# One up tile per chunk gets its exact rest from an accumulating transfer instead of a VectorE subtraction

## The chip, the cores and the metric

The kernel runs on one core of a Trainium2 chip. The metric is the device time of one execution, in microseconds. The core has five engines that run their own instruction queues in order and wait for each other through semaphores: TensorE (PE, matmuls; PEld is its weight load), VectorE (DVE), ScalarE (ACT), GpSimd (POOL) and SyncE (SP). SyncE, ScalarE and GpSimd can issue transfers, which 16 DMA engines carry out.

## The reference

Two layers of a residual trunk over 256 tokens of width 2048, in float32. Each layer has a mixer (two groups of attention heads between an input and an output projection) and a feed-forward part. The change touches the feed-forward part only:

```
h = rms_norm(x, pre_ffn_norm[l])                       # 256 x 2048
f = (silu(h @ w_gate[l]) * (h @ w_up[l])) @ w_down[l]  # 2048 -> 5632 -> 2048
x = x + rms_norm(f, post_ffn_norm[l])
```

## The kernel before

Every product is made of rounded parts. A float32 matrix W is split into hi, W rounded to TensorE's reduced format (float32r), and lo = W - hi, the exact rest, which fits that format too. With the activations split in the same way (sh, sl), a product is three matmuls: sh hi, sh lo, sl hi (`product`, lines 922 to 927).

All weights lie in DRAM in the order in which they are used (`weight_order`, `weights_laid_out`), as tiles of 128 partitions by 2 by 512 float32 values, 512 KB each. `fetch` (line 184) issues the loads on SyncE's queue into one of four `raw` buffers (line 202); `feed` (line 240) splits a tile, with ScalarE rounding it to `hi` (line 250) and VectorE subtracting (line 252, `lo`). `hi` and `lo` have six buffers each. `weights(i, ahead)` feeds four tiles ahead of the one that TensorE is to use (LOOKAHEAD = 4).

Gate and up: the 5632 hidden columns are cut into 11 chunks (c = 0 to 10) of 512. In each chunk the 2048 rows are taken as eight row pairs kp of 256 rows, and each pair has a gate tile and an up tile, so a chunk uses 16 tiles: gate and up of kp 0, then of kp 1, and so on. Four of the row pairs (kp 2, 4, 5 and 6; 4 and 6 in chunk 0) are done by `seven`, a 2-by-2 block product with seven instead of eight block products. Its up tile `T` is the sum of the up tile and half of the gate tile; that sum is made by a transfer: the up tile is loaded by SyncE (line 210), and GpSimd then issues a transfer that adds the first half of the gate tile to it on its way into the buffer (line 211, `accum_op`, 256 KB). `mixed_weights` (lines 216 to 238) makes the further sums on VectorE (lines 232, 233) and splits them (lines 225, 226, into `Th`, `Tl`, `hi`, `lo`). The other four row pairs are done by `eight` (line 1035), 24 matmuls with the plain `hi` and `lo` of the gate and up tiles. Row pair 1, which the change concerns, is one of these, from chunk 1 on in every chunk.

At the end of a chunk, `shared_part` (lines 959 to 966) combines what the seven products share (ScalarE line 962, VectorE lines 963 to 966) out of the banks of PSUM that the next chunk then needs, and lines 1079 to 1082 apply SiLU, the row scale and the product of gate and up. The results are transposed on TensorE some ticks later (`flip`, line 1084).

The order of the instructions on each engine is made when the kernel is built: a scheduler lists the instructions by priorities, and each engine then runs its list in order. A wait at the head of a list holds everything behind it. GpSimd's list in this stage holds nothing but the accumulating transfers; SyncE's holds the loads.

Of the kernel before, what the change touches and what calls it, by code (L numbers as in the profile page):

```python
# [10 lines left out]
F32R = mybir.dt.float32r  # L11
BF16 = mybir.dt.bfloat16
AF = mybir.ActivationFunctionType
ALU = mybir.AluOpType
# [3 lines left out]
P = 128  # L18
D = 2048
S = 256  # L20
L = 2
# [3 lines left out]
FF = 5632  # L25
CW = 512
# [29 lines left out]
def weight_order():  # L56

    order = []

    def queue_pair(name, l, kp, c):  # L60
        order.append((name, l, kp, c))
        return len(order) - 1

    plan = []
    sevens, plain = set(), set()
    for l in range(L):
        lay = {"in": {}, "o": {}, "gate": {}, "up": {}, "down": {}}
        for n, (ca, cb) in enumerate(PAIRS):
            for kp in IN_ORDER if n else range(KT // 2):
                lay["in"][ca, kp] = queue_pair("w_in", l, kp, ca)  # L70
                lay["in"][cb, kp] = queue_pair("w_in", l, kp, cb)
                if kp in IN_NOW[n]:
                    plain.add(lay["in"][cb, kp])
        order_o = [(c, kp) for kp in KP_O for c in (0, 1)]
        order_o += [(c, kp) for c in (2, 3) for kp in range(KT // 2)]
        lay["order_o"] = order_o
        for c, kp in order_o:
            lay["o"][c, kp] = queue_pair("w_o", l, kp, c)
        for c in range(FF // CW):
            for kp in FIRST_ORDER if c == 0 else range(KT // 2):  # L80
                lay["gate"][c, kp] = queue_pair("w_gate", l, kp, c)
                lay["up"][c, kp] = queue_pair("w_up", l, kp, c)
                if kp in (FIRST_SEVEN if c == 0 else SEVEN):
                    sevens.add(lay["up"][c, kp])
        for half in range(2):
            for kp in range(FF // P // 2):
                for c in (2 * half, 2 * half + 1):
                    lay["down"][c, kp] = queue_pair("w_down", l, kp, c)
                if kp in DOWN_SEVEN:
                    sevens.add(lay["down"][2 * half + 1, kp])  # L90
        plan.append(lay)
    return order, plan, sevens, plain
# [48 lines left out]
def kernel(  # L141
# [15 lines left out]
    nc = tc.nc  # L157
    const = ctx.enter_context(tc.tile_pool(name="const", bufs=1))
    small = ctx.enter_context(tc.tile_pool(name="small", bufs=4))
    wpool = ctx.enter_context(tc.tile_pool(name="wpool", bufs=1))  # L160
# [14 lines left out]


    order, plan, sevens, plain = weight_order()
    stream = [weights_in_turn[i].rearrange("p (k n) -> p k n", k=2) for i in range(len(order))]

    ready = {}  # L180
    raws, loads = [], []
    fed = [0]

    def fetch(upto):
        while len(raws) < min(upto, len(stream)):
            i = len(raws)
            for j in range(i, min(i + EARLY + 1, mix_raw[3])):
                if j in sevens and j not in sums:
                    summed(j)
            if i in sevens:  # L190
                raws.append(sums[i])
                continue
            if i + 1 in sevens:
                g = mix_raw[0].tile([P, 2, CW], F32, tag="G", bufs=mix_raw[1], name=f"G{i}")
                loads.append(nc.sync.dma_start(g, stream[i]))
                raws.append(g)
                continue
            if i in plain or i + 1 in plain:
                raw = mix_pool[0].tile([P, 2, CW], F32, tag="GU", bufs=4, name=f"GU{i}")
            else:  # L200
                raw = wpool.tile([P, 2, CW], F32, tag="raw", bufs=4, name=f"raw{i}")
            loads.append(nc.sync.dma_start(raw, stream[i]))
            raws.append(raw)
# [3 lines left out]
    def summed(i):  # L207

        sums[i] = mix_raw[0].tile([P, 2, CW], F32, tag="T", bufs=mix_raw[2], name=f"T{i}")
        loads.append(nc.sync.dma_start(sums[i], stream[i]))  # L210
        nc.gpsimd.dma_start(sums[i][:, 0, :], stream[i - 1][:, 0, :], accum_op=ALU.add)  # L211
# [4 lines left out]
    def mixed_weights(i):  # L216

        g, u = raws[i - 1], raws[i]
        hi = wpool.tile([P, 2, CW], F32R, tag="hi", bufs=6, name=f"hi{i}")
        lo = wpool.tile([P, 2, CW], F32R, tag="lo", bufs=6, name=f"lo{i}")  # L220
        th = mix_pool[0].tile([P, 3, CW], F32R, tag="Th", bufs=1 if i in plain else 2, name=f"Th{i}")
        tl = mix_pool[0].tile([P, 3, CW], F32R, tag="Tl", bufs=1 if i in plain else 2, name=f"Tl{i}")

        def split(h, l, w):
            nc.scalar.activation(h, w, AF.Copy)  # L225
            nc.vector.tensor_tensor(out=l, in0=w, in1=h.bitcast(F32), op=ALU.subtract)  # L226

        if i in plain:
            nc.vector.tensor_tensor(out=u[:, 0, :], in0=g[:, 0, :], in1=u[:, 0, :], op=ALU.add)
        split(hi, lo, u)  # L230
        t2 = u[:, 1, :]
        nc.vector.tensor_tensor(out=t2, in0=t2, in1=u[:, 0, :], op=ALU.subtract)  # L232
        nc.vector.tensor_tensor(out=g, in0=g, in1=t2.unsqueeze(1).to_broadcast([P, 2, CW]), op=ALU.add)  # L233
        split(th[:, 2, :], tl[:, 2, :], t2)
        split(th[:, 0:2, :], tl[:, 0:2, :], g)
        t1, b22 = ((hi[:, k, :], lo[:, k, :]) for k in range(2))
        t3, t4, t2 = ((th[:, k, :], tl[:, k, :]) for k in range(3))
        return {"b22": b22, "t1": t1, "t2": t2, "t3": t3, "t4": t4}

    def feed(upto):  # L240
        fetch(upto)
        while fed[0] < min(upto, len(stream)):
            i = fed[0]
            raw = raws[i]
            if i in sevens or i in plain:
                ready[i] = mixed_weights(i)
                fed[0] += 1
                continue
            hi = wpool.tile([P, 2, CW], F32R, tag="hi", bufs=6, name=f"hi{i}")
            nc.scalar.activation(hi, raw, AF.Copy)  # L250
            lo = wpool.tile([P, 2, CW], F32R, tag="lo", bufs=6, name=f"lo{i}")
            rest = nc.vector.tensor_tensor(out=lo, in0=raw, in1=hi.bitcast(F32), op=ALU.subtract)  # L252
            ready[i] = (hi, lo)
            fed[0] += 1
            rests.append(rest)
# [11 lines left out]
    def weights(i, ahead):  # L267
        feed(i + 1 + ahead)
        return ready[i]
# [702 lines left out]
    for l in range(L):  # L972
# [29 lines left out]
        with tc.manual_schedule(engines={mybir.EngineType.Activation, mybir.EngineType.DVE}):  # L1002
            feed(idx + 6)
            for kp in range(4, 8):
                unit(accs, mix, idx + kp - 4, kp, (0,), False, kp == 7, 0)
            evac_chunk(pool, accs[0], mg, ssm, gpost, 3, 0, f"o{l}")
            rescale(mg, ssm, 0, f"o{l}")
            for kp in range(4, 8):
                feed(idx + 3 + kp)
                fetch(min(idx + 8 + kp, idx + 12))  # L1010
                unit(accs, mix, idx + kp - 4, kp, (1,), False, kp == 7, 0)
                transposed(0, 32 + l * KT, xT, cols=(kp - 4,))
# [90 lines left out]
        for half in range(2):  # L1103
# [69 lines left out]
            for t in range(NT):  # L1173
# [4 lines left out]
                for c in cc:  # L1178
                    for kp in range(nkp - tail, nkp):
# [3 lines left out]
                        hi, lo = weights(plan[l]["down"][c, kp], LOOKAHEAD)  # L1183
# [67 lines left out]
```

## Time and profile before

| | |
|---|---|
| time, median of 3 runs | 2214.32 us (2211.67 to 2216.69) |
| profiled execution | 2215.14 us, span 2213.4 us, granted clock 0.998 |
| busy in the span | TensorE 99%, VectorE 84%, ScalarE 61%, GpSimd 6% |
| transfers | 466.73 MB, mean 211 GB/s |
| subtraction lo (line 252), from raw tiles | 534 times, mean 1223 ns |
| rounding hi (line 250), from raw tiles | 534 times, mean 1053 ns |
| issue of an accumulating transfer (line 211) | 108 times, mean 873 ns; lands after 3.7 / 6.7 / 9.4 us (least, median, most) |
| load of a 512 KB raw tile | 534 times, lands after 4.7 us (median) |

How to read the profile: busy time is the time in which an engine has an instruction at work; instructions are pipelined, so two that follow each other closely overlap a little. A releaser, written after an arrow, is what ended an idle time. The DMA share is how much of the time the 16 DMA engines had a packet at work, on average.

### The profile page before, as it was taken

To read this page: it belongs to the slowest core of one execution; us is meant where nothing else is said; L and a number is where in the kernel's file an instruction comes from. 1 tells how busy PE (TensorE), PEld (TensorE's weight loads), DVE (VectorE), ACT (ScalarE), POOL (GpSimd) and SP (SyncE) were. 2 spreads that over 40 slices of the span, in tenths; PEclk is the share of its full clock that TensorE was granted. 3 is DMA by queue.
4 is the path that set the end of the run, shared out by engine and by line. 5 is a ranking of instruction groups with operands and counts; after the bars stand their busy time and mean duration, and the time that the engine had idled before them with its cause. 6 is when DMAs were issued, how large, how long until landed. Compare 5 with 4: busy or idle time off the path is not lost.

```text
span 2213.4 us, 28454 instructions
## 1 busy us (share of the span) xinstructions
PE 2185.5 (99%) x10009; PEld 1790.9 (81%) x10009; DVE 1864.0 (84%) x2548; ACT 1354.6 (61%) x2030; POOL 142.2 (6%) x184
## 2 busy tenths in 40 slices
PE   9999999999999999999999999999999999999998
PEld 7788888778888888888888888887788888888886
DVE  7888655899999998989788886559999999999897
ACT  7566664656656656656565656646666556566564
POOL 1200000000000000000011000000000000000000
PEclk9999999999999999999999999999999999999999
DMA  8654555776776775767465545558677677667672
GB/s 304 208 180 153 190 176 186 250 237 215 218 256 211 211 258 180 241 215 240 157 239 190 177 160 177 174 187 268 208 225 235 224 221 238 226 204 243 200 254 98
DMA packets 138079, 466.73 MB, mean 211 GB/s; under 512 B 15824, under 2 KB 16336, under 8 KB 137424
## 3 DMA queue, kind: packets, MB, share of 16 engines
q1 hardware_dynamic: 120512, 430.30, 56.3%
q0 software_dynamic: 15552, 28.32, 7.5%
q10 hardware_dynamic: 1872, 6.31, 0.7%
q8 instruction: 78, 1.28, 0.2%
q14 instruction: 65, 0.53, 0.1%
HBM read 456.47 MB, written 8.39 MB: 210 GB/s over the span
## 4 chain that ended last, share of the span: by engine, by line
PE 78%; DVE 11%; DMA 4%; issue 3%; ACT 3%; SPq 0%; DVEq 0%; ACTq 0%
PE c L925 7%; PE c L926 7%; PE c L927 7%; PE in L925 5%; PE in L927 5%; PE in L926 5%; PE dn L1136 5%; PE dn L1135 5%; PE dn L1138 5%; DVE lo L252 3%; DMA raw<-in_weights_in_turn_dram 3%; PE o L464 3%; PE o L466 3%; PE o L465 3%; DVE Tl L226 2%
## 5 line engine op out<-in xcount | busy, mean ns | idle before, releaser
L252 DVE TENSOR_TENSOR lo<-raw,hi 128x1024 fp32r<-128x1024 f32 x534 | 643.3, 1223 | 161.4 <-ACT hi L250 161.2
L250 ACT ACTIVATE hi<-raw 128x1024 fp32r<-128x1024 f32 x534 | 552.4, 1053 | 235.1 <-DMA raw<-in_weights_in_turn_dram 63.5
L925 PE MATMUL c<-hi,xF 128*128 128x512 f32 x820 | 321.8, 395 | 6.2 <-DVE w L966 4.0
L926 PE MATMUL c<-lo,xF 128*128 128x512 f32 x820 | 320.0, 391 | 0.0
L927 PE MATMUL c<-hi,xF 128*128 128x512 f32 x820 | 318.3, 390 | 0.0
L211 POOL DMA_DIRECT2D T<-in_weights_in_turn_dram x108 | 94.3, 873 | 1669.3 <-PE c L926 520.9
L925 PEld LDWEIGHTS c<-hi,xF 128*128 128x128 f32 x820 | 153.7, 188 | 40.8 <-DVE w L966 6.3
L1135 PE MATMUL dn<-hi,jh 128*128 128x512 f32 x464 | 180.7, 389 | 0.0
L1136 PE MATMUL dn<-lo,jh 128*128 128x512 f32 x464 | 180.5, 389 | 0.0
L926 PEld LDWEIGHTS c<-lo,xF 128*128 128x128 f32 x820 | 154.1, 188 | 32.0 <-DVE lo L252 1.6
L927 PEld LDWEIGHTS c<-hi,xF 128*128 128x128 f32 x820 | 153.9, 188 | 32.1
L252 DVE TENSOR_TENSOR lo<-G,hi 128x1024 fp32r<-128x1024 f32 x108 | 131.7, 1220 | 26.7 <-ACT hi L250 26.6
L225 ACT ACTIVATE Th<-T 128x512 fp32r<-128x512 f32 x108 | 67.8, 627 | 138.6 <-DVE T L232 126.7
L1138 PE MATMUL dn<-hi,jl 128*128 128x512 f32 x464 | 142.9, 389 | 0.0
L226 DVE TENSOR_TENSOR lo<-T,hi 128x1024 fp32r<-128x1024 f32 x108 | 131.7, 1220 | 10.9 <-ACT hi L225 10.3
L226 DVE TENSOR_TENSOR Tl<-G,Th 128x1024 fp32r<-128x1024 f32 x108 | 131.8, 1220 | 9.6 <-ACT Th L225 9.6
L225 ACT ACTIVATE hi<-T 128x1024 fp32r<-128x1024 f32 x108 | 113.4, 1050 | 40.4 <-PE c L927 19.9
L225 ACT ACTIVATE Th<-G 128x1024 fp32r<-128x1024 f32 x108 | 113.9, 1054 | 36.6 <-DVE G L233 35.2
L233 DVE TENSOR_TENSOR G<-G,T 128x1024 f32<-128x1024 f32 x108 | 132.0, 1222 | 2.1
L925 PE MATMUL in<-hi,xT 128*128 128x512 f32 x328 | 131.5, 402 | 0.5 <-ACT hi L738 0.5
L925 PE MATMUL in<-hi,xI 128*128 128x512 f32 x328 | 131.3, 402 | 0.2 <-ACT xI L383 0.2
L926 PE MATMUL in<-lo,xT 128*128 128x512 f32 x328 | 128.2, 391 | 1.0 <-DVE lo L252 0.8
(376 smaller groups left out, 4660.2 us busy)
## 6 DMA issues: line engine op xcount, KB each, us to landing
raw<-in_weights_in_turn_dram SPq DMA_DIRECT2D x534, 512.0 KB, 4.7
T<-in_weights_in_turn_dram SPq DMA_DIRECT2D x108, 512.0 KB, 4.7
G<-in_weights_in_turn_dram SPq DMA_DIRECT2D x108, 512.0 KB, 4.8
T<-in_weights_in_turn_dram POOLq DMA_DIRECT2D x108, 256.0 KB, 6.7
GU<-in_weights_in_turn_dram SPq DMA_DIRECT2D x32, 512.0 KB, 4.6
away_ffn<-x ACTq DMA_DIRECT2D x8, 512.0 KB, 6.1
xd<-away_ffn SPq DMA_DIRECT2D x8, 512.0 KB, 9.2
xr<-in_x_columns_dram SPq DMA_DIRECT2D x8, 256.0 KB, 6.7
```

The source lines that it names most:

```text
L211: nc.gpsimd.dma_start(sums[i][:, 0, :], stream[i - 1][:, 0, :], accum_op=ALU.add)
L225: nc.scalar.activation(h, w, AF.Copy)
L226: nc.vector.tensor_tensor(out=l, in0=w, in1=h.bitcast(F32), op=ALU.subtract)
L233: nc.vector.tensor_tensor(out=g, in0=g, in1=t2.unsqueeze(1).to_broadcast([P, 2, CW]), op=ALU.add)
L250: nc.scalar.activation(hi, raw, AF.Copy)
L252: rest = nc.vector.tensor_tensor(out=lo, in0=raw, in1=hi.bitcast(F32), op=ALU.subtract)
L925: nc.tensor.matmul(a, sh, hi, start=first, stop=False)
L926: nc.tensor.matmul(a, sh, lo, start=False, stop=False)
L927: nc.tensor.matmul(a, sl, hi, start=False, stop=last)
L1135: nc.tensor.matmul(accs[c, t], sh, hi[:, kk, :], start=first, stop=False)
L1136: nc.tensor.matmul(accs[c, t], sh, lo[:, kk, :], start=False, stop=False)
L1138: nc.tensor.matmul(accs[c, t], sl, hi[:, kk, :], start=False, stop=last)
```

## The change

For 20 tiles (the up tile of row pair 1 in chunks 1 to 10 of both layers), the rest is no longer made by VectorE. ScalarE writes the rounded tile twice: once negated, into `lo`, and once as it is, into `hi`. Then GpSimd issues a transfer that reads the same tile again from DRAM, all 512 KB, and adds it onto `lo`, so that `lo` becomes W - hi. These tiles are no longer in `rests`, the list that orders the making of the sums in chunk 0; nothing in later chunks uses it.

```diff
     order, plan, sevens, plain = weight_order()
+    added = {plan[l]["up"][c, 1] for l in range(L) for c in range(1, FF // CW)}
...
             hi = wpool.tile([P, 2, CW], F32R, tag="hi", bufs=6, name=f"hi{i}")
+            lo = wpool.tile([P, 2, CW], F32R, tag="lo", bufs=6, name=f"lo{i}")
+            if i in added:
+                nc.scalar.activation(lo, raw, AF.Copy, scale=-1.0)
             nc.scalar.activation(hi, raw, AF.Copy)
-            lo = wpool.tile([P, 2, CW], F32R, tag="lo", bufs=6, name=f"lo{i}")
+            if i in added:
+                nc.gpsimd.dma_start(lo, stream[i], accum_op=ALU.add)
+                ready[i] = (hi, lo)
+                fed[0] += 1
+                continue
             rest = nc.vector.tensor_tensor(out=lo, in0=raw, in1=hi.bitcast(F32), op=ALU.subtract)
             ready[i] = (hi, lo)
             fed[0] += 1
```

## The prediction

> **What bounds the kernel now.** I read the page's busy shares first, then the same shares in stretches cut at the ends of the gate-and-up chunks, then who the TensorE waited for, then the instructions around one such wait.
>
> ```profile
> span 2213.4 us, 28454 instructions
> PE 2185.5 (99%) x10009; PEld 1790.9 (81%) x10009; DVE 1864.0 (84%) x2548; ACT 1354.6 (61%) x2030; POOL 142.2 (6%) x184
> ...
> q1 hardware_dynamic: 120512, 430.30, 56.3%
> q0 software_dynamic: 15552, 28.32, 7.5%
> ...
> T<-in_weights_in_turn_dram POOLq DMA_DIRECT2D x108, 256.0 KB, 6.7
> ```
>
> TensorE has work 99% of the span at granted clock 0.998, so no change to the other engines can win more than its few gaps; a late operand can lose any amount. The last line is the nearest relative of the new transfer: an accumulating transfer of half its size lands after 6.7 us at the median.
>
> By chunk, layer 0 (stretches from the last gate-or-up matmul of one chunk to that of the next; columns: length, then busy us of PE, PEld, DVE, ACT, POOL, then the clock, the DMA share, GB/s):
>
> ```profile
> 446.70:490.50 43.80, 42.43 (x190) 34.37 (x189) 43.09 (x55) 27.40 (x32) 3.24 (x5) 1.00 0.67 202
> 490.50:535.10 44.60, 42.49 (x190) 34.25 (x189) 39.05 (x45) 26.27 (x31) 3.92 (x5) 1.00 0.75 241
> ...
> 662.20:703.90 41.70, 41.70 (x189) 34.55 (x188) 39.00 (x43) 25.31 (x30) 3.49 (x4) 1.00 0.72 229
> ```
>
> A settled chunk is 41.7 us with TensorE never idle and VectorE busy 39.0 of them. The chunks numbered 1 and 2 take 2.1 and 2.9 us more; 3 and 4 (42.7 each in the same answer) 1.0 each. So 7 us per layer are all there is to win in the stage that the change touches, and most of it is in the first two chunks that it touches. Who TensorE waited for from 445 to 580 us, and the place of the longest wait:
>
> ```profile
> PE c L925 <- DVE w L966: 2.1, 1, 2.1
> PE p L925 <- ACT Th L225: 1.0, 1, 1.0
> PE q L925 <- ACT sh L937: 0.4, 1, 0.4
> ```
> ```profile
> 492.78 1.06 ACT L250 ACTIVATE hi<-raw 128x1024 fp32r<-128x1024 f32 x1 [3.51 <-DMA raw<-in_weights_in_turn_dram]
> ```
> ```profile
> 493.87 1.23 DVE L252 TENSOR_TENSOR lo<-raw,hi 128x1024 fp32r<-128x1024 f32 x1 [2.74 <-ACT hi L250]
> 495.01 0.68 DVE L965 TENSOR_TENSOR w<-q,w 128x512 f32<-128x512 f32 x1
> 495.61 0.68 DVE L966 TENSOR_TENSOR w<-q,w 128x512 f32<-128x512 f32 x1
> ```
>
> Counted through the built order, the raw tile at 492.78 is exactly the one that the change handles in chunk 2 (up, row pair 1). Its load lands late, VectorE stands in order behind it, the two shared sums L965 and L966 stand behind that, and TensorE waits 2.1 us for the bank that they free. Layer 1 shows the same once (1.9 us between 1545 and 1680 us).
>
> **The change part by part.**
>
> *Taken from VectorE:* 20 subtractions of 1223 ns (row L252), 24.5 us. Where VectorE is not late, this is worth nothing, since TensorE is full. In chunk 2 it takes the late tile out of VectorE's queue: L965 and L966 need not wait. Gain 2.1 us in layer 0, 1.9 in layer 1.
>
> *Added to ScalarE:* 20 copies of 1053 ns (row L250), 21.1 us. ScalarE is busy 25.3 of 41.7 us in a settled chunk: cover enough, no cost by itself. But the transfer can start only after the copy. In the built order the negative comes ahead of the rounding copy in settled chunks and behind it in chunk 2, where it ends at 492.78 + 2 × 1.0 = 494.8. Behind it on ScalarE stand the next tile's rounding (needed by TensorE 10 us later) and the SiLU: 1 us each way, covered by the same 10 us.
>
> *The raw tile* comes free when ScalarE is done (494.8) and not VectorE (495.1): SyncE's next load moves by nothing.
>
> *Added to GpSimd's queue:* 20 issues of 868 ns, 17.4 us on an engine 6% busy. In the built order each new transfer stands behind the four T accumulates of its own chunk and ahead of those of the next. The next T accumulate after 490.06 is issued at 512.21, so nothing behind is held. In front it matters:
>
> ```profile
> 490.06 0.86 POOL L211 DMA_DIRECT2D T<-in_weights_in_turn_dram  x1 [4.29 <-DMA T<-in_weights_in_turn_dram]
> 512.21 0.86 POOL L211 DMA_DIRECT2D T<-in_weights_in_turn_dram  x1 [21.28 <-DVE T L232]
> ```
>
> In chunk 2 the fourth T accumulate is already out; the new issue comes at 494.8 plus 0.7 (a T load issued at 693.63 lands after 6.2 us, and its accumulate goes at 700.50), 495.5. In a settled chunk the fourth one goes at 700.50, after the copy (698.65 + 1.06 = 699.7), so the new one goes at 701.4.
>
> *The transfer itself.* Both transfers then fall into a time in which the DMA engines are full:
>
> ```profile
> 490.00:499.00 9.00, 6.89 (x31) 5.39 (x30) 6.26 (x10) 4.59 (x5) 0.86 (x1) 1.00 1.01 348
> 499.00:504.00 5.00, 5.00 (x28) 4.16 (x27) 5.00 (x7) 2.59 (x5) 0.00 (x0) 1.00 0.05 22
> ```
> ```profile
> 700.00:706.00 6.00, 6.00 (x29) 4.95 (x28) 5.83 (x9) 2.94 (x4) 0.86 (x1) 1.00 1.01 353
> 706.00:712.00 6.00, 6.00 (x28) 4.99 (x27) 5.93 (x7) 3.18 (x5) 0.00 (x0) 1.00 0.04 9
> ```
>
> Work in engine time, from the queue rows: q0 takes 7.5% of 2213.4 us for 108 transfers of 256 KB, 1.54 us each; a 512 KB one is twice that, 3.1 us of all 16 engines (a plain 512 KB load: 56.3% × 2213.4 us × 0.524 / 430.3 MB = 1.5). A full burst is lengthened by that much, whatever the order within it. The bursts end at about 499.2 and 706.2. The T accumulate of 700.50 lands 6.9 us later, at 707.4, which is 1.2 after its burst's end; allowing 0 to 1.2 us for that, the tile is complete at 499.2 + 3.1 = 502.3 to 503.5 in chunk 2 and at 709.3 to 710.5 in the settled one. TensorE's first matmul with it stands at 499.43 and at 710.52. So chunk 2 gets it 2.9 to 4.1 us too late, settled chunks just in time. Queued behind that matmul is everything on TensorE.
>
> Bounds for chunk 2: the quickest T accumulate landed after 3.7 us; with 1.5 us for the second half, 495.5 + 5.2 = 500.7, 1.3 late. At the contention of 490.06 (7.7 us for 256 KB) it is 495.5 + 9.2 = 504.7, 5.3 late. I take 3.0, the low end of the burst reading: that is the row of the same place and time, and the 1.0 us gaps of chunks 3 and 4 give some of a larger delay back. Settled chunks: 0 to 1.2 us to spare, gone at an engine time of 4.3 us instead of 3.1 at the latest.
>
> Chunk 1: copy done at 448.7, issue 449.4, burst full until 455.0 (share 0.91 from 446 to 455, then 0.04); complete at 458.1 to 459.3, say 458.5. TensorE came there at 451.92, and now comes 8 matmuls (8 × 0.227 = 1.8 us) later, because the built order puts other products ahead: 4.8 late. That delay is not lost on top: VectorE, busy in every us there, catches up in it, so that the 2.1 us of gaps in chunk 1 and the 2.1 us at L966 vanish inside it, and at chunk 2's first use TensorE stands at 499.43 + 4.8 - 2.1 - 2.1 = 500.0, still ahead of 502.3. Chunk 2 decides. Chunk 3 by the same reading is 2.1 late against the old time and chunk 4 about 1, both less than the shift already there.
>
> Sum: 3.0 us per layer, two layers, 6.0. The profiled execution is 2215.14 us (span 2213.4 and 1.7 around it), 0.8 above the median shown: 2215.1 + 6.0 = 2221.1; against the median 2214.3 + 6.0 = 2220.3. I give 2220.5.
>
> By the Trainium skill, "DMA: Bandwidth & Descriptors", the section on the anatomy of a GpSimd DMA, such a transfer takes about 2.0 us plus its bytes over 436 GB/s. For 512 KB that is 3.2 us as an estimate, and the tile would be there at 498.7, before its use; for 256 KB it gives 2.6, where the trace has 3.7 to 9.4. The same page (section on SWDGE, HWDGE and iDMA) says that a transfer into float32r always casts, and gives no rate for that. No row here shows it: the T tiles are plain float32.
>
> **The rivals.**
>
> *Hidden (faster, 0.18).* The transfer lands in time everywhere. It needs 495.5 + x below 497.1 (499.43 less the vanished 2.1) plus what chunk 1 has shifted, so x of 4 to 5 us; only T accumulates in idle stretches (3.7) come near, and these move half the bytes. Then the 2.1 and 1.9 us go, and up to 7 us per layer if lighter VectorE work mends chunks 1 to 4 wholly: 2214.3 - 4 to - 8, 2206 to 2210. The page's fit above would have it so.
>
> *Late in every chunk (slower, 0.20).* If the accumulate into a rounded-type tile costs 4.5 to 5 us of engine time, each of the 16 settled chunks waits 1 to 1.5 us more, 16 to 24, with 5 per layer from the early ones: 2240 to 2248. Against it: the T accumulates are added by the same engines at 1.54 us per 256 KB, and by that price the settled chunks are just in time. For it: the spare is about 1 us at most, and the type is another.
>
> *Cancelled (same, 0.10).* The lower bound holds, 1.3 late in chunk 2, and chunks 3 and 4 give back their 2 us: 2212 to 2216.
>
> **How the numbers follow.** 0.2% is 4.4 us, about what a measurement can tell from no change. The forecast case (late in chunks 1 and 2 alone, +2 to +10) has 0.52, of which 0.12 lies within 4.4 us. Faster 0.18; same 0.12 + 0.10 = 0.22; slower 0.40 + 0.20 = 0.60. The range leaves out the far half of the first and of the second rival: 2209 to 2237. The forecast case alone is 2216 to 2224.
>
> **What would show it.** Right: TensorE waits on a DMA into lo, 3 to 5 us each, twice per layer, in chunks 1 and 2; no wait for L966 in chunk 2; settled chunks stay at 41.7 us; VectorE busy some 24 us less, ScalarE 21 more; q0's share up by 2.8 points; new transfers landing after 7 to 9 us. Wrong: waits on lo in settled chunks (second rival), or none at all and chunk 2 under 43 us (first). It would also fall if the burst's end itself moved, since every landing time above hangs on it.

## The result and the profile after

The changed kernel takes 2237.8 us (median; 2235.0 to 2241.2), the kernel before on the same chip 2214.1. The ratio is 1.0107, interval 1.0088 to 1.0127: slower by 23.7 us, where 6.0 was forecast and 2237 was the top of the range. The profiled execution took 2239.4 us, its span 2237.7.

The page of the changed kernel, its busy times, its software DMA queue and the row of the new transfers:

```profile
span 2237.7 us, 28507 instructions
PE 2193.3 (98%) x10009; PEld 1798.6 (80%) x10009; DVE 1843.3 (82%) x2528; ACT 1375.0 (61%) x2050; POOL 157.6 (7%) x204
...
q0 software_dynamic: 18432, 38.81, 9.9%
```
```profile
lo<-in_weights_in_turn_dram POOLq DMA_DIRECT2D x20, 512.0 KB, 9.0
```

The amounts of work are those of the forecast: VectorE 20.7 us less (1864.0 to 1843.3), ScalarE 20.4 more, q0 from 7.5% to 9.9%, twenty transfers that land after 9.0 us at the median. None of these says where 24 us went. The chunks of layer 0 do (columns as for the chunks before: length, busy us of PE, PEld, DVE, ACT and POOL, granted clock, DMA share, GB/s). The rows are chunks 1, 2, 3 and 6:

```profile
446.20:496.10 49.90, 44.45 (x190) 36.01 (x189) 41.24 (x52) 28.45 (x33) 4.17 (x5) 0.93 0.68 192
496.10:546.60 50.50, 44.94 (x190) 36.33 (x189) 41.97 (x48) 28.03 (x33) 5.23 (x6) 0.93 0.77 231
546.60:590.90 44.30, 42.09 (x190) 34.55 (x189) 38.06 (x43) 27.40 (x32) 5.25 (x6) 1.00 0.81 242
674.60:716.60 42.00, 42.00 (x190) 34.52 (x189) 37.96 (x43) 26.23 (x31) 4.39 (x5) 1.00 0.80 240
```

Chunk 1 grew from 43.8 to 49.9 us, chunk 2 from 44.6 to 50.5, chunk 3 from 42.7 to 44.3; the later ones take 41.7 to 42.7. Layer 1 is the same: 44.2 to 50.0, 44.5 to 50.1, 42.8 to 43.2. From the end of chunk 4 to the end of chunk 10 layer 0 takes 252.1 us (250.5 before) and layer 1 251.5 (250.5). The loss is in the first three chunks that the change touches.

Two things in these rows differ from the forecast. Chunk 1 keeps its loss and chunk 2 adds its own. And the mean granted clock is 0.93 in both, where it had been 1.00 in every chunk. TensorE's waits over the whole span, then the two waits of layer 0 beside the issue of the second transfer:

```profile
PE c L935 <- DMA lo<-in_weights_in_turn_dram: 25.9, 9, 5.6
```
```profile
449.17 0.86 POOL L257 DMA_DIRECT2D lo<-in_weights_in_turn_dram  x1 [2.26 <-ACT lo L254]
...
458.13 0.79 PE L935 MATMUL c<-lo,xF 128*128 128x512 f32 x1 [5.09 <-DMA lo<-in_weights_in_turn_dram]
...
500.69 0.88 POOL L257 DMA_DIRECT2D lo<-in_weights_in_turn_dram  x1 [2.86 <-ACT lo L254]
...
508.34 0.79 PE L935 MATMUL c<-lo,xF 128*128 128x512 f32 x1 [5.56 <-DMA lo<-in_weights_in_turn_dram]
```

The transfers landed 9.0 and 7.6 us after their issue. Layer 1 waits 5.1 and 5.4 us at the same places, chunk 3 waits 2.2 and 1.1. The wait for L966 in chunk 2 is gone, as forecast. Now the stretch around the first wait, cut where TensorE stops, where the clock changes and where work resumes:

```profile
449.00:452.90 3.90, 3.90 (x18) 3.00 (x16) 3.90 (x9) 3.87 (x5) 0.86 (x1) 1.00 0.99 287
452.90:455.90 3.00, 0.14 (x1) 0.00 (x0) 3.00 (x8) 2.35 (x3) 0.00 (x0) 1.00 1.06 289
455.90:458.10 2.20, 0.00 (x0) 0.00 (x0) 0.83 (x1) 0.00 (x0) 0.00 (x0) 0.50 0.46 101
458.10:462.70 4.60, 4.57 (x13) 3.69 (x14) 0.00 (x0) 0.75 (x2) 0.00 (x0) 0.50 0.02 4
462.70:467.00 4.30, 4.30 (x23) 3.54 (x22) 3.90 (x5) 2.96 (x5) 0.00 (x0) 1.00 0.00 0
```

Read two columns. The clock falls to 0.50 at 455.9, 2.9 us after the last matmul's end, and stays there for 6.8 us. For 4.6 of these TensorE works again: 13 matmuls, where the next stretch, at 1.00, has 23 in 4.3. Thirteen at that pace would take 2.4 us, so the fall costs some 2.2 beyond the wait. The other column is VectorE (the third busy time): it works 3.0, then 0.83, then nothing, and the DMA share falls to 0.02. VectorE does not catch up in the wait; it stops with TensorE. The chain that stops it, on ScalarE and VectorE:

```profile
454.21 1.04 ACT L255 ACTIVATE hi<-raw 128x1024 fp32r<-128x1024 f32 x1
461.95 0.59 ACT L1098 COPY act<-actT_ps 128x512 f32<-128x512 f32 x1 [6.70 <-PE actT_ps L1097]
462.43 0.63 ACT L946 ACTIVATE sh<-s 128x512 fp32r<-128x512 f32 x1
```
```profile
463.10 0.69 DVE L948 TENSOR_TENSOR sl<-s,sh 128x512 fp32r<-128x512 f32 x1 [6.37 <-ACT sh L946]
```

ScalarE copies the transposes of chunk 0's output (L1098). TensorE makes these behind the matmul that waits for the transfer, so the copy waits too, and the rounding of the token sums (L946) stands behind the copy. VectorE stands 6.4 us for that rounding, and behind it are all subtractions. Raw tiles are then freed and loaded later: raw163, the tile that chunk 2 hands to its transfer, was loaded at 485.4 in the kernel before and at 490.6 here.

### The profile page after: what moved, and what is told of

Read it like the earlier page. It is cut to its first block, busy times and chain, and to the rows that moved or that the text cites. A ratio compares the mean times of both kernels' runs of the same rounds, so it can differ in the third digit from the quotient of the medians.

```text
span 2237.7 us, 28507 instructions
## 1 busy us (share of the span) xinstructions
PE 2193.3 (98%) x10009; PEld 1798.6 (80%) x10009; DVE 1843.3 (82%) x2528; ACT 1375.0 (61%) x2050; POOL 157.6 (7%) x204
## 4 chain that ended last, share of the span: by engine, by line
PE 80%; DVE 8%; DMA 6%; ACT 3%; issue 3%; SPq 0%; POOL 0%; DVEq 0%; ACTq 0%; POOLq 0%
PE c L935 7%; PE c L936 7%; PE c L934 7%; PE in L934 6%; PE in L935 6%; PE in L936 6%; PE dn L1147 5%; PE dn L1145 5%; PE dn L1144 5%; DMA lo<-in_weights_in_turn_dram 4%; PE o L473 3%; PE o L475 3%; PE o L474 3%; DVE lo L261 2%; PE p L935 2%
## 5 line engine op out<-in xcount | busy, mean ns | idle before, releaser
L261 DVE TENSOR_TENSOR lo<-raw,hi 128x1024 fp32r<-128x1024 f32 x514 | 618.3, 1221 | 144.2 <-ACT hi L255 143.8
L935 PE MATMUL c<-lo,xF 128*128 128x512 f32 x820 | 324.5, 396 | 25.9 <-DMA lo<-in_weights_in_turn_dram 25.9
```

What stands on the lines that cost most here:

```text
L935: nc.tensor.matmul(a, sh, lo, start=False, stop=False)
```

## The experiments

The theory at the start: the loss is made of late transfers in the first chunks alone, their waits add, and the clock falls after the long ones. Its rivals: a price of 1.2 us on each of the 20 transfers; and the prediction's own, that chunk 1's delay is taken back and chunk 2 decides.

**The late chunks alone.** The transfer only in chunks 4 to 10:

```diff
-    added = {plan[l]["up"][c, 1] for l in range(L) for c in range(1, FF // CW)}
+    added = {plan[l]["up"][c, 1] for l in range(L) for c in range(4, FF // CW)}
```

> The changed kernel, but with the tile given its rest by a transfer only in chunks 4 to 10 of each layer (14 transfers in place of 20; chunks 1 to 3 stay as in the kernel before). Theory (the loss is made by the transfers that land late, and those are all in chunks 1 to 3): the traces of before and after show chunks 4 to 10 of layer 0 shifted by +12.1 at the end of chunk 4 and +13.7 at the end of chunk 10, and those of layer 1 by +23.3 and +24.3, so 14 transfers cost together +1.6 and +1.0 us: 2214 to 2218 us, no wait over 1 us on lo, and a granted clock of 1.0 throughout. Rival (each of the 20 transfers costs the same, 23.7/20 = 1.2 us, by taking GpSimd, the DMA engines or the tiles' memory from others): 14 x 1.2 = +16.6, 2231 us.

Measured: 2218.7 us, ratio 1.0016 (1.0006 to 1.0025), +3.6 us, 0.7 above the theory's range and far below the rival's 2231. The clock stayed at 1.00 through chunks 1 to 10 of both layers. The waits are 2.3 and 1.3 us in chunk 4, now the first with a transfer, and small after that (TensorE's waits, two longest groups):

```profile
PE c L935 <- DMA lo<-in_weights_in_turn_dram: 4.5, 4, 2.3
PE c L934 <- DVE w L975: 3.9, 4, 1.5
```

Fourteen transfers cost 3.6 us together: no steady price of 1.2 us each. But my "no wait over 1 us" was wrong for the first one in each layer.

**Chunk 1 alone, chunk 2 alone, and both** (the line is shown for the first; the others have `(2,)` and `(1, 2)`):

```diff
-    added = {plan[l]["up"][c, 1] for l in range(L) for c in range(1, FF // CW)}
+    added = {plan[l]["up"][c, 1] for l in range(L) for c in (1,)}
```

> The transfer in chunk 1 of each layer alone (2 transfers). Theory (waits add; nothing behind the waiting TensorE catches up): chunk 1 loses what it lost in the changed kernel, +6.2 us in layer 0 (end of chunk 0 at -0.9, end of chunk 1 at +5.3) and +5.7 in layer 1, made of a wait of 5.25 us on lo and one fall of the granted clock to 0.5 after it, less what the chunk lost before; chunk 2 keeps its length of 44.6 and 44.5. Sum 2 x 5.3 to 6.2: 2225 to 2227 us. Rival (the prediction: what chunk 1 loses is taken back by VectorE, which is late in chunk 2 by 2.1 us and would not be): the wait in chunk 1 shows but chunk 2 is shorter by what VectorE gained: 2214 to 2218 us.

> The transfer in chunk 2 of each layer alone (2 transfers). Theory (waits add): chunk 2 loses +5.9 us in layer 0 and +5.6 in layer 1, as it did in the changed kernel (44.6 to 50.5, 44.5 to 50.1), with a wait of some 5.6 us on lo, a granted clock of 0.5 for 6.8 us after it, and no wait at the shared sums: 2224 to 2226 us. Rival (the prediction's step: the transfer of chunk 2 lands 2.9 to 4.1 us late when chunk 1 has not slipped, and the wait of 2.1 us at the shared sums goes): a wait of 3 to 5 us, +3.0 per layer net, 2220 us, with no fall of the clock if the wait stays under about 3 us.

> The transfers of chunks 1 and 2 of each layer and no others (4 transfers). Alone, those of chunk 1 gave +5.3 us and those of chunk 2 +6.9. Theory (a delay of TensorE in chunk 1 holds back the loads of chunk 2 by as much, so chunk 2 pays in full after chunk 1 has paid): the sum or more, 2227 to 2235 us, with two waits of over 5 us per layer. Rival (the prediction: chunk 2 decides, chunk 1's delay is inside it): as chunk 2 alone, 2220 to 2223 us.

Measured: chunk 1 alone 2220.4 us, 1.0030 (1.0018 to 1.0041), +5.3; chunk 2 alone 2221.9, 1.0038 (1.0023 to 1.0053), +6.9; both 2232.1, 1.0091 (1.0075 to 1.0108), +18.0, inside the theory's range. Chunk 1 alone missed both of its expectations: it lies between them. Both together cost 5.8 us more than the sum, 12.2, the opposite of chunk 1's loss being inside chunk 2's. The 5.8 itself is hardly beyond the noise of three runs, whose intervals are 2.5 to 3.7 us to each side. The traces show more directly that the losses add: chunk 2 takes 50.1 and 49.8 us (layers 0 and 1) with its own transfer alone, and 49.8 and 50.1 behind a late chunk 1. The run with both has all four long waits:

```profile
PE c L935 <- DMA lo<-in_weights_in_turn_dram: 20.3, 4, 5.5
```

Chunk 2 alone tests the prediction's central step most directly, as chunk 1 is undisturbed there (chunks 1 and 2, then the issue and the wait):

```profile
446.50:490.30 43.80, 42.44 (x190) 34.28 (x189) 42.77 (x54) 27.39 (x32) 3.17 (x5) 1.00 0.67 210
490.30:540.40 50.10, 44.71 (x190) 36.23 (x189) 38.92 (x44) 27.68 (x32) 4.79 (x6) 0.93 0.74 228
```
```profile
494.20 0.86 POOL L257 DMA_DIRECT2D lo<-in_weights_in_turn_dram  x1 [3.47 <-ACT lo L254]
...
502.05 0.80 PE L935 MATMUL c<-lo,xF 128*128 128x512 f32 x1 [5.39 <-DMA lo<-in_weights_in_turn_dram]
```

The tile was complete at 502.0; the prediction had 502.3 to 503.5. TensorE came to it at 496.7 and not 499.4, since the wait at L966 was gone. So the net lateness is 502.0 - 499.4 = 2.6 us, close to the 3.0 forecast; yet the chunk grew by 5.5 (44.6 to 50.1). The rest, 2.9 (2.4 if one allows for this execution's start of the chunk some 0.5 us earlier), is what the fall of the clock has left to explain (mean 0.93 in the row above, 1.00 there before). The theory's range for this run, 2224 to 2226, was 2 to 4 us high, as chunks 3 and 4 gave 0.8 us back in layer 0 and 1.8 in layer 1.

Chunk 1 alone shows how much is given back after a delay. From the ends of the chunks, each against the kernel before: layer 0 was 6.0 us later at the end of chunk 1 than at the end of chunk 0, 7.2 after chunk 2, 5.6 after chunk 4; layer 1 6.3, 5.0 and 3.4. So something is given back, 0.4 us in layer 0 and 2.9 in layer 1, neither all nor nothing. In layer 0 chunk 2 kept the wait at the shared sums (1.9 us; L975 here is L966 before), and the subtraction of raw163 came at 498.9, in the kernel before at 493.9: the feed had slipped by as much as TensorE. The clock even fell again behind that wait, for a shorter time (two stretches of 5 us):

```profile
500.00:505.00 5.00, 3.63 (x11) 2.85 (x12) 5.00 (x9) 3.76 (x5) 0.00 (x0) 0.74 0.77 269
505.00:510.00 5.00, 5.00 (x26) 4.15 (x25) 5.00 (x6) 1.04 (x3) 0.00 (x0) 0.92 0.09 21
```

**The clock by itself.** TensorE is kept busy through the waits with products that add zero:

```diff
+    zero = const.tile([P, P], F32R, name="zero")
+    nc.vector.tensor_scalar_mul(zero, ident, 0.0)
...
+                        if c in (1, 2) and kp == 1 and kk == t == 0 and col == 1:
+                            for n in range(24):
+                                nc.tensor.matmul(banks[0], zero, g[0][:, 0, :], start=False, stop=False)
```

> The changed kernel with 24 products of 128x512 by a matrix of zeros put on TensorE just ahead of the first product that reads the transferred tile, in chunks 1 and 2 of each layer (they add nothing to the sums). By the row of such products, 0.21 us each, they fill 5.1 us of the wait of 5.25 to 5.7. Theory (the clock falls because TensorE stands still, and the fall costs time beyond the wait): no row of the granted clock at 0.5 after the four waits, the waits on lo under 1 us, and the four falls' price of 2.3 to 2.8 us each gone: 2237.8 - 4 x 2.3 to 2.8 = 2227 to 2229 us. Rival (the falls come anyway, or cost nothing since the feed is late by as much): 2237 to 2240 us.

Measured: 2225.3 us, 1.0056 (1.0041 to 1.0071), 12.5 us under the changed kernel and 1.7 below the theory's range, though TensorE does 22 us of useless work (96 products, one every 0.233 us). The granted clock is 1.00 in every chunk (chunks 1, 2 and 3 of layer 0):

```profile
445.70:494.20 48.50, 47.94 (x213) 38.83 (x213) 45.54 (x58) 31.86 (x37) 5.24 (x6) 1.00 0.80 242
494.20:541.50 47.30, 47.30 (x214) 39.04 (x213) 37.91 (x42) 26.28 (x31) 4.37 (x5) 1.00 0.71 216
541.50:583.30 41.80, 41.80 (x190) 34.60 (x189) 37.97 (x43) 26.34 (x31) 4.39 (x5) 1.00 0.79 238
```

That is more than the clock: the filler also moved the built order, and chunk 3 lost its wait (44.3 to 41.8). Chunk 1, ahead of which the two kernels hardly differ, is the cleaner pair. It went from 49.9 to 48.5 us, with 5.6 us of filler and 0.6 of wait in place of 5.1 of wait. So the fall had cost 1.4 + 1.1 = 2.5 us there, near the 2.2 read from the stretch above. In layer 1 it is 50.0 to 47.9.

The same filler with the transfer in chunk 1 alone:

> The transfer in chunk 1 of each layer alone, with the 24 products by zeros in chunk 1: the pair to that kernel without them, which took 2220.4 us with waits of 5.2 us and a granted clock of 0.5 for 6.8 us in each layer. Theory (a fall of the clock costs 0.5 x 4.6 us = 2.3 us, the part of its 6.8 us in which TensorE works again): 2220.4 - 2 x 2.3 = 2215.8, 2215 to 2217 us. Rival (the fall costs nothing, as the feed is late by as much): 2219 to 2221 us.

Measured: 2213.2 us, 0.9996 (0.9987 to 1.0006), below both expectations: 7.2 us less than without the filler, and level with the kernel before. Chunk 1 shrank from 49.7 to 48.0 us (layer 1: 50.5 to 47.8), mean 2.2, about the clock's share. (The expectation's 6.8 us at half clock holds for layer 1; after chunk 1's wait in layer 0 it was 3.4.) The rest was won in chunk 2, which has no wait left:

```profile
445.60:493.60 48.00, 47.99 (x214) 38.88 (x213) 46.10 (x59) 30.46 (x36) 5.18 (x6) 1.00 0.81 249
493.60:535.30 41.70, 41.70 (x189) 34.55 (x189) 39.35 (x44) 25.81 (x30) 3.48 (x4) 1.00 0.74 234
```

VectorE is busy 46.1 of chunk 1's 48.0 us (42.4 of 49.7 without the filler). In this built order ScalarE's L946 is ahead of the copy, T149's rounding is ahead of hi152's, and raw163's load is ahead of T173's, which it follows in the kernel before. So a delay of TensorE can be taken back by chunk 4, as the prediction assumed, but only where the feed keeps running through it. How much of this is the order and how much the clock, this pair does not separate.

**What stops the feed.** The transposes of chunk 0's output put off, so that L946 is not behind the copy; then, as a control, the same edit in the kernel before:

```diff
-            start(flip(), DEFER_ACT)
+            start(flip(), DEFER_ACT + 4 * (c == 0))
```

> The changed kernel with all its 20 transfers, and the transposes of chunk 0's output (with ScalarE's copies of them, L1098) put off by four steps, so that in the built order ScalarE's rounding L946 of the token sums no longer stands behind a copy that waits for TensorE. In the changed kernel TensorE's wait in chunk 1 held that copy until 461.95, L946 behind it until 462.43, and VectorE's subtraction L948 behind that until 463.10: VectorE stood still from 456.7 to 463.1 and all loads of chunk 2 came later by that. Theory (this chain, and not the number of buffers, handed the delay of chunk 1 on to chunk 2): VectorE works through the wait, the loads of chunk 2 come some 5 us sooner against TensorE, the wait on lo in chunk 2 is under 2 us without a fall of the clock, that of chunk 1 stays at 5 us with one. Of the 23.7 us chunk 1's 5 to 6 per layer stay, less the gaps that chunks 2 to 4 had before: 2217 to 2226 us. Rival (buffers that TensorE frees hold the loads back): two waits over 5 us per layer as before, 2234 to 2240 us.

> The control: the kernel before, without transfers, with the same four steps' delay of chunk 0's transposes. In its built order T173's load still stands ahead of raw163's and the late subtraction ahead of the shared sums. Theory (the chain costs only when TensorE waits long; here its longest wait in chunk 1 is 1.0 us): the wait at the shared sums of chunk 2 stays at 1 to 2 us, 2211 to 2216 us. Rival (putting the transposes off is itself worth the gain): 2205 to 2210 us, and then it is no test of the transfer's delay.

Measured: 2235.8 us, 1.0101 (1.0085 to 1.0116), with waits of 5.0, 4.9, 4.5 and 3.6 us. The control took 2211.3 us, 0.9987 (0.9978 to 0.9996), with both waits at L966 still there (4.1 us in all), so the edit does not hide a large gain of its own. My theory fell and the rival stands. VectorE worked on, L948 at 456.8, but only until 462.6. ScalarE was held by the next thing, the rounding of tile 152:

```profile
455.78 0.63 ACT L946 ACTIVATE sh<-s 128x512 fp32r<-128x512 f32 x1 [0.38 <-DVE s L944]
464.84 1.06 ACT L255 ACTIVATE hi<-G 128x1024 fp32r<-128x1024 f32 x1 [8.43 <-PE c L936]
```

There are six `hi` buffers. Tile 152 needs the one of tile 146, which TensorE reads until behind its wait. Everything queued behind that rounding on ScalarE waits with it, T149's rounding at 469.9 too, and T165's load came at 471.3 us (462.8 in the run with the filler, where T149's rounding stood ahead). In the changed kernel the same rounding ran at 464.95, so the copy there only hid this second hold. No run had more `hi` buffers, so this second hold is read from the trace and not tested by itself.

**The tile of row pair 3**, needed 12 us later in the chunk:

```diff
-    added = {plan[l]["up"][c, 1] for l in range(L) for c in range(1, FF // CW)}
+    added = {plan[l]["up"][c, 3] for l in range(L) for c in range(1, FF // CW)}
```

> The change made with the up tile of row pair 3 in place of row pair 1: the same 20 transfers of 512 KB, the same 20 copies less on VectorE, but this tile is needed some 13 us later in the chunk. Theory (only late landing costs; a transfer as such is free): TensorE waits for no transfer over 1 us, the clock stays at 1.0, the wait at the shared sums stays (the tile of row pair 1 is VectorE's again): 2212 to 2217 us. Rival (each transfer costs 1.2 us by GpSimd, the DMA engines or the memory, 20 of them): 2231 to 2239 us.

Measured: 2224.9 us, 1.0057 (1.0045 to 1.0070). Both expectations missed: chunk 1 waits 4.7 and 4.4 us, chunk 3 2.5 and 1.8, and the clock falls again.

```profile
461.11 0.85 POOL L257 DMA_DIRECT2D lo<-in_weights_in_turn_dram  x1 [15.18 <-ACT lo L254]
...
469.97 0.80 PE L935 MATMUL c<-lo,xF 128*128 128x512 f32 x1 [4.73 <-DMA lo<-in_weights_in_turn_dram]
```

Its use is 12 us later, and so is its issue: in the built order the negative copy stands at 459.7 on ScalarE, 6 us behind the tile's rounding, with the copies of the transposes between. The landing is 8.9 us again. Chunks 5 to 10 cost 0.1 and 0.6 us more than before: in a settled chunk this transfer too is free.

**Half the tile.** The second half of the pair by transfer, the first by VectorE:

```diff
-                nc.scalar.activation(lo, raw, AF.Copy, scale=-1.0)
+                nc.scalar.activation(lo[:, 1, :], raw[:, 1, :], AF.Copy, scale=-1.0)
...
-                nc.gpsimd.dma_start(lo, stream[i], accum_op=ALU.add)
...
+                nc.gpsimd.dma_start(lo[:, 1, :], stream[i][:, 1, :], accum_op=ALU.add)
+            own = slice(0, 1) if i in added else slice(0, 2)
```

> The change with half a tile: the rows of the pair's second half (256 KB) get their rest by the transfer, those of the first half by VectorE. In the built order TensorE needs the second half 14 matmuls (some 3 us) after the first, and the queue rows give the halved transfer 1.4 us less of all engines: 4 to 5 us more to spare in all, where the changed kernel's waits are 5.1 to 5.6. Theory (lateness alone costs): the waits on the transfer in chunks 1 and 2 are under 1.5 us each, no fall of the granted clock, the waits at the shared sums come back at 1 to 2 us as a half subtraction of 0.68 us stands ahead of them: 2213 to 2218 us. Rival (half the cost for half the bytes): 2224 to 2228 us.

Measured: 2213.1 us, 0.9997 (0.9988 to 1.0006), as the theory had it, with its waits a little longer (2.0 and 1.9 us in chunk 1, none over 1 in chunk 2) and one fall of the clock of 3.4 us in layer 0:

```profile
PE c L933 <- DMA lo<-in_weights_in_turn_dram: 3.9, 2, 2.0
PE c L932 <- DVE w L973: 2.9, 3, 1.4
```

Halving the bytes and gaining 3 us of slack together took away all of the 23.7 us; the run does not separate the two.

**The gain half alone.** The kernel before, with the shared sums given priority over the subtractions; then that together with the halved transfer:

```diff
-                    shared_part(extra, w)
+                    with tc.high_priority(offset=URGENT):
+                        shared_part(extra, w)
```

> The kernel before, without any new transfer; the four shared sums of gate and up are given priority over the subtractions, so that in the built order L965 and L966 of chunk 2 stand ahead of the two tiles' subtractions behind which TensorE waited 2.1 us in layer 0 and 1.9 us in layer 1. This is the gain that the change was forecast to have (step 'Taken from VectorE'), by itself. Theory (that wait is real time and nothing takes its place): 2215 - 2.1 - 1.9 = 2211, 2209 to 2213 us, chunk 2 shorter by 2 us. Rival (the late tile's subtraction itself becomes the wait, as TensorE comes to it 2 us sooner): 2214 to 2216 us, with a wait on lo of 1 to 2 us in chunk 2.

> The halved transfer together with the priority of the shared sums. Theory (the wait at the shared sums is the only gain there is, and the halved transfer is free): as the priority alone gives, 2209 to 2213 us. Rival (VectorE's lighter load is worth time of its own, in chunks 3 and 4, which had 1 us of gaps each): 2 to 4 us below the priority alone. Rival (the halved transfer waits once the gap ahead of it is gone): 2 to 4 us above it.

Measured: 2209.3 us, 0.9983 (0.9974 to 0.9992), 4.6 us faster than before and faster than either kernel. The wait for L966 in chunk 2 is gone, but chunk 1 has grown (chunks 1 and 2 of layer 0; 43.8 and 44.6 us before):

```profile
446.90:492.50 45.60, 43.55 (x190) 34.45 (x190) 44.91 (x57) 27.47 (x33) 4.26 (x5) 1.00 0.69 206
492.50:534.90 42.40, 42.40 (x189) 34.31 (x189) 39.71 (x44) 26.43 (x31) 3.54 (x5) 1.00 0.77 245
```

Together the two chunks take 88.0 us against 88.4, and in layer 1 88.6 against 88.7. The rest of the gain lies elsewhere in the traces: 0.7 and 1.1 us in chunks 3 and 4, and 1.5 between the gate-and-up stages of the two layers, where the run with chunk 1 alone gained as much. So the priority wins about what was forecast, but the run does not show that the wait in chunk 2 was what it won.

With the halved transfer added it is 2213.2 us, 0.9999 (0.9991 to 1.0008): the second rival, as the gap that had covered the halved transfer is gone and TensorE waits 7.9 us for it in four places. As large a gain as the forecast saw in the change is had by a priority, without any transfer.

## Why the prediction was wrong

- **The gain** (VectorE's late tile taken out of the queue, 2.1 + 1.9 us): the wait is gone in the changed kernel, as forecast. What that was worth no run shows by itself: the priority wins 4.6, but chunk 1 takes back nearly all that it wins in chunk 2.
- **ScalarE, GpSimd and the raw tile at nothing**: right as costs of their own; the work moved as forecast. ScalarE's place in the loss is another: it hands TensorE's stop on.
- **The transfer lands with the end of the burst** (502.3 to 503.5 in chunk 2, 458.1 to 459.3 in chunk 1): right within 0.3 us, 502.0 (chunk 2 alone) and 458.1; the wait in chunk 1 was to be 4.8 and was 5.1. Engine time: 9.9% of 2237.7 us less 7.5% of 2213.4, over 20 transfers, is 2.8 us each; 3.1 was forecast.
- **Settled chunks just in time**: right, 41.7 to 42.7 us; chunks 5 to 10 cost 1.6 and 1.0 us in all. The rival "late in every chunk" came near the measured time with the wrong place. The rival "hidden" needed a landing after 4 to 5 us; none of the 20 came under 7.6.
- **"Chunk 2 decides", 3.0 us per layer**: the term for chunk 2 was right as lateness (2.6 measured) and mis-sized as time, by the clock, which I had at 1.00 throughout: chunk 2 alone grew its chunk by 5.5.
- **"That delay is not lost on top: VectorE, busy in every us there, catches up in it"**: the step that failed. VectorE stood for 6.4 us behind ScalarE, which waited for TensorE: at the copy of the transposes, and with that moved, at a buffer that TensorE still read. Chunk 1 alone costs 5.3 us, and chunk 2 then repeats its wait in full, as its load had slipped from 485.4 to 490.6.

By the runs, +23.7 is: chunk 1 5.3, chunk 2 6.9, the two together 5.8 more, and 5.7 for chunks 3 to 10 on top (3.6 when chunks 4 to 10 stand alone); the last two are differences of runs with intervals of some 3 us to each side. Cut by mechanism, the four falls at 2.2 to 2.9 us are 9 to 12 of it; the rest is waits, less the gaps that they replace. Late transfers in chunks 1 and 2 were the right place and the right cause; missing were the second price of each wait and the engine that hands it on.

## What to carry to other kernels

Before a wait of TensorE is called absorbed, follow each other engine's queue from that moment: the first instruction that reads TensorE's output or needs a buffer that it frees stops all behind it, loads included. A wait of some 5 us had a second price in the clock here, 2 to 3 us, and filling such waits with useless products was cheaper than leaving TensorE idle (by 7.2 us with the transfer in chunk 1 alone, the changed order included). Where an engine's queue holds back something urgent, changing the order (4.6 us won here) comes before moving the work to another engine.

## What was not expected of the hardware

In the changed kernel the granted clock fell to 0.50 after each of the four waits of 5.1 to 5.6 us, and each time for 6.8 us. The length of the wait alone does not decide it. With the transfer in chunk 1 alone, the wait of 5.2 us was followed by 3.4 us of it in layer 0 and by 6.8 in layer 1, and a wait of 1.9 us by 3.4. With half the tile, a wait of 2.0 us was followed by 3.4; the wait of 2.2 us in chunk 3 of the changed kernel had none. The Trainium skill, "TensorE: Matmul & The Clock Gate", Part 1, tells of a window of about 3.4 us that runs freely, of half rate after an idle window, and advises against gaps of TensorE over about 3.4 us. The lengths of 3.4 and 6.8 us here are one and two such windows, and the trace agrees; but falls after waits of 1.9 and 2.0 us show that much shorter gaps can be followed by half rate too.

The traces also show that the window runs freely. Within each execution the falls start whole multiples of 3.413 us apart: in the changed kernel 51.20, 1061.55 and 51.20 us, which are 15, 311 and 15 of them. Here are two windows of that grid, the one ahead of the first fall and the one that holds most of chunk 3's wait, which no fall follows:

```profile
452.47:455.88 3.41, 0.57 (x3) 0.14 (x1) 3.41 (x9) 2.78 (x4) 0.00 (x0) 1.00 1.06 300
551.47:554.88 3.41, 1.51 (x7) 0.93 (x5) 3.34 (x5) 3.40 (x4) 0.00 (x0) 1.00 0.62 124
```

TensorE is busy 0.57 us of the first and 1.51 of the second, 0.17 and 0.44 of them. Counted so, from 380 to 2190 us of all fourteen traces (where one has no fall there, its grid is taken from the fall behind the last matmul), each of the 24 falls follows a window with TensorE busy 0.51 or less of it, and no other window at full clock is under 0.44. So what counts here is how much of one window a wait empties, about half being the limit, and a wait of 2 us costs nothing or 3.4 us at half clock by where it falls.

A 512 KB transfer that accumulates into a rounded-type tile took 2.8 us of the engines' time (above); a plain load of that size took 1.5. It landed after 9.0 us at the median, and half of one after 7.7: 1.3 us less, about the engine time of the half left out (1.4). The other 7.7 us the two share; in the stretch from 449.0 to 455.9 above, while the first one was on its way, the engines were full (shares 0.99 and 1.06).
